# Column means in two float32r passes, and the key-low passes of two heads on separate row halves of TensorE's array

## The chip, the cores and the metric

One core of a Trainium2 chip runs the whole kernel. The metric is the device time of one execution in microseconds, taken as the median of several runs. The engines that matter are TensorE (PE in the profile: matmuls and transposes; PEld: its weight loads), VectorE (DVE), ScalarE (ACT) and GpSimd (POOL). They run side by side and wait for one another only at semaphores. TensorE multiplies a stationary operand, loaded into an array of 128 x 128, with a moving operand of up to 512 columns.

## The reference

Two layers of a decoder trunk over 512 tokens of width 1024, all in float32. In each layer a normalized input is projected once, and four branches read the projection: a short convolution, sparse attention (DSA), a chunkwise linear recurrence (HGRN2) and cross-attention to 256 memory tokens. The branches are lifted to the model's width, gated, summed and projected, and a SwiGLU feed-forward part follows. What the change touches is three things.

```python
def rmsnorm(x, g):
    y = xf * lax.rsqrt(jnp.mean(xf * xf, axis=-1, keepdims=True) + EPS)
    ...
# index scores of the sparse attention, 8 heads of 64, one common key ik:
rel = jax.nn.relu(jnp.einsum('bthd,bsd->bths', iqb, ik) * idx_scale)
score = jnp.einsum('bths,bth->bts', rel, iwb)
...                                   # the 128 best keys of each token
# attention over them, 8 heads of 64, one common key k:
logits = jnp.einsum('bthd,btkd->bthk', qb, k_sel) * att_scale
p = jax.nn.softmax(logits, axis=-1)
...
# HGRN2 output, 4 heads of 128:
o_c = rmsnorm(o_c, hgrn_out_norm) * jax.nn.silu(g_g)
```

## The kernel before

**Float32 by float32r.** TensorE takes operands in float32 or in float32r (a rounded float32). The kernel splits most operands in two float32r parts, `hi` (a ScalarE copy, L97 in the profile, since the helper `A` records every ScalarE instruction) and `lo` (VectorE's difference of the value and `hi`). A product is then the three passes `hi*hi`, `hi*lo`, `lo*hi` (`mm3`, L270 to L272). Weight chunks are split in this way too (L225). These projections are by far the most of the work: 512 columns of activations a pass in `features`, or 256 columns of weights a pass in `tokens`.

**Column means.** Norms over features that lie on the partitions need a mean down the columns of a 128x512 tile. The kernel takes it by a matmul with a constant matrix, `ones_d` (1/1024) or `ones_h` (1/128), in plain float32: `norm_feature` (L301, three times: ahead of each feed-forward part, and between the layers) and the end of each HGRN2 `head` (L972, four heads in two layers). `norm_token` (L309) takes means of the same sums of squares in another form and isn't touched.

**Scores.** `dots` makes the scores of one head for one block of 128 tokens against `n` keys, where `n` is 128 times the block's number (128 to 512). The query tile of a head (`qS` for attention, `iqS` for the index) has `hi` in partitions 0 to 63 and `lo` in 64 to 127, written by `heads_T`. The key's `hi` (`kS[0]`, `ikS[0]`) stands in both halves, written by `twin`; the key's `lo` stands in the lower half only, with zeros in the other, which GpSimd sets. So the first pass (L685) gives `q_hi*k_hi + q_lo*k_hi`, and the second (L686) `q_hi*k_lo`, both over all 128 rows of the array and into one PSUM tile "at". There are two "at" banks. In `select` (blocks 1 to 3) ScalarE reads an index score with Relu, and VectorE adds it up; `attend` (blocks 0 to 3) has VectorE add the mask and take the maximum, and ScalarE the exponential. Then the probabilities are transposed (L709) and multiplied with the values (L715): this product writes two heads' results to the two column halves of the array, 64 columns each.

**Order.** The kernel's generators are woven together by hand (`script`, `weave`): the steps of `select` and `attend` stand between steps of `lift` and of the branches' projections, so that TensorE has matmuls to do while other engines work on a head. The final order on each engine is made at build time by a scheduler that simulates the engines; TensorE then runs its instructions in that order. Other small matmuls in the text below: L937 to L965 (HGRN2 products, of which L939 uses 64 columns) and L331, a transpose of a tile with only four rows (the positions).

Of the kernel before, what the change touches and what calls it, by code (L numbers as in the profile page):

```python
# [13 lines left out]
F32R = mybir.dt.float32r  # L14
I32 = mybir.dt.int32
U8 = mybir.dt.uint8
AF = mybir.ActivationFunctionType
# [4 lines left out]
P = 128  # L22
S = 512
# [5 lines left out]
HD = 64  # L29
# [40 lines left out]
def hybrid_trunk(ctx: ExitStack, tc: tile.TileContext, x, mem, positions, norm_mix, w_in, conv_w,  # L70
# [3 lines left out]
    act, dve, pe, pool = nc.scalar, nc.vector, nc.tensor, nc.gpsimd  # L74

    consts = ctx.enter_context(tc.tile_pool(name="consts", bufs=1))
    start = ctx.enter_context(ExitStack())
# [7 lines left out]
    order = mybir.DependencyInfo(mybir.DependencyClass.NoSync, mybir.DependencyReason.DATA)  # L85
# [4 lines left out]
    def A(dst, src, func, **kw):  # L90
        name = tables.get(func)
        if name is not None and name != table["set"]:
            load = act.preload_act_table_set(name)
            for u in table["users"]:
                tc.add_manual_dep(load.ins, u.name, order, reason="table set")
            table.update(set=name, load=load.ins, users=[])
        i = act.activation(dst, src, func, **kw)  # L97
        if name is not None:
            tc.add_manual_dep(i.ins, table["load"].name, order, reason="table set")
            table["users"].append(i.ins)  # L100
        return i
# [4 lines left out]
    def at_ps():  # L106
        return pat.tile([P, 512], F32, name="at", bufs=AT_BUFS)
# [4 lines left out]
    def f(ap):  # L112
        return ap.bitcast(F32)
# [3 lines left out]
    ones_d = consts.tile([P, P], F32, name="ones_d")  # L117
    dve.memset(ones_d, 1.0 / D)
    ones_h = consts.tile([P, P], F32, name="ones_h")
    dve.memset(ones_h, 1.0 / P)  # L120
    eps = consts.tile([P, 1], F32, name="eps")
    dve.memset(eps, EPS)
    half = consts.tile([P, 1], F32, name="half")
# [18 lines left out]
    ps = tr_ps()  # L142
# [16 lines left out]
    ps = tr_ps()  # L159
# [136 lines left out]
    def scratch512(n):  # L296
        return state.tile([P, S], F32, name="sq", bufs=2)[:, :n]

    def norm_feature(ssq):
        ps = tr_ps()  # L300
        pe.matmul(ps, ones_d, ssq, start=True, stop=True)  # L301
        r = state.tile([P, S], F32, name="rstd", bufs=1)
        rstd(r, ps, scratch512(S), scratch512(S))
        return r
# [196 lines left out]
    def mixer(l, h, norms, cm, cf):  # L501
# [174 lines left out]
        with pool_("dsa") as dp:  # L676
            qS = dp.tile([P, 8, S], F32R, name="qS")
            kS = (dp.tile([P, S], F32R, name="k_hi"), dp.tile([P, S], F32R, name="k_lo"))
            pool.memset(f(kS[1][HD:P, :]), 0.0)
            vt = dp.tile([P, NT, HD], F32, name="vt")  # L680
            biases = [causal_bias] + [dp.tile([P, (t + 1) * P], F32, name=f"bias{t}") for t in range(1, NT)]

            def dots(ps, q, k, hh, t, n):
                s = slice(t * P, (t + 1) * P)
                pe.matmul(ps, q[:, hh, s], k[0][:, :n], start=True, stop=False)  # L685
                pe.matmul(ps, q[:, hh, s], k[1][:, :n], start=False, stop=True)  # L686

            def attend(t, dp2, y_b):
                n = (t + 1) * P
                s = slice(t * P, (t + 1) * P)  # L690
                for q in range(2):
                    probs = []
                    for i in range(4):
                        ps = at_ps()[:, :n]
                        dots(ps, qS, kS, 4 * q + i, t, n)
                        p = dp2.tile([P, S], F32, name="prob", bufs=PR_BUFS)[:, :n]
                        mx, sm = small(1), small(1)
                        dve.tensor_tensor_reduce(out=p, in0=ps, in1=biases[t], scale=-1.0, scalar=-OFF * 4,  # L698
                                                 op0=OP.add, op1=OP.min, accum_out=mx)
                        A(p, p, AF.Exp, bias=mx, scale=-1.0, accum_out=sm)  # L700
                        dve.reciprocal(sm, sm)
                        A(p, p, AF.Copy, scale=sm)
                        probs.append(p)
                    pt = dp2.tile([P, NT, S], F32, name="pt", bufs=PT_BUFS)
                    for b in range(t + 1):
                        pp = tr_ps()
                        for e in range(2):
                            for i in range(2):
                                pe.transpose(pp[:, (2 * e + i) * P:(2 * e + i + 1) * P],  # L709
                                             probs[2 * i + e][:, b * P:(b + 1) * P], ident)  # L710
                        A(pt[:, b, :], pp, AF.Copy)
                    pv = tr_ps()[:, :2 * P]
                    for b in range(t + 1):
                        for e in range(2):
                            pe.matmul(pv[e * HD:(e + 1) * HD, :], vt[:, b, :], pt[:, b, e * 2 * P:(e + 1) * 2 * P],  # L715
                                      start=b == 0, stop=b == t)
                    pv = pv.rearrange("p (a b) -> p a b", b=P)
                    hi, lo = (y_b[x][:, 2 * q:2 * q + 2, s] for x in range(2))
                    A(hi, pv, AF.Copy)
                    dve.tensor_sub(lo, pv, f(hi))  # L720
                    yield

            with pool_("idx") as ip:
                iqS = ip.tile([P, 8, S], F32R, name="iqS")
                ikS = (ip.tile([P, S], F32R, name="ik_hi"), ip.tile([P, S], F32R, name="ik_lo"))
                pool.memset(f(ikS[1][HD:P, :]), 0.0)
                iw = ip.tile([P, NT, 8], F32, name="iw")

                def rope(u, heads, t):
# [21 lines left out]
                def heads_T(dst, h0, u, heads, t):  # L751
                    ps = tr_ps()[:, :heads * HD]
                    for i in range(heads // 2):
                        pe.transpose(ps[:, i * P:(i + 1) * P], u[:, i * P:(i + 1) * P], ident)  # L754
                    ps = ps.rearrange("p (a b) -> p a b", b=P)
                    s = slice(t * P, (t + 1) * P)
                    for e in range(2):
                        d = dst[:, h0 + e:h0 + heads:2, s]
                        src = ps[e * HD:(e + 1) * HD]
                        A(d[0:HD], src, AF.Copy)  # L760
                        dve.tensor_sub(d[HD:P], src, f(d[0:HD]))

                def unit(ps, t, c0, heads):
                    u = ip.tile([P, 4, HD], F32, name="unit", bufs=3)[:, :heads]
# [3 lines left out]
                def twin(ps, t, c0, norm, dst):  # L768
                    u = ip.tile([P, 2, HD], F32, name="twin", bufs=2)
                    A(u[:, 0, :], ps[:, c0:c0 + HD], AF.Copy, scale=r_t[:, t:t + 1])  # L770
                    if norm:
                        headnorm(u[:, 0:1], 1, gk_b[l])
                    rope(u[:, 0:1], 1, t)
                    dve.tensor_copy(u[:, 1, :], u[:, 0, :])
                    ps = tr_ps()[:, :P]
                    pe.transpose(ps, u.rearrange("p a b -> p (a b)"), ident)
                    s = slice(t * P, (t + 1) * P)
                    A(dst[0][:, s], ps, AF.Copy)
                    dve.tensor_sub(dst[1][0:HD, s], ps[0:HD], f(dst[0][0:HD, s]))

                def iq_part(ps, t, c0, heads, h0):
                    u = unit(ps, t, c0, heads)
# [24 lines left out]
                def select(t):  # L807
                    n = (t + 1) * P
                    score = ip.tile([P, S], F32, name="score", bufs=1)[:, :n]
                    for hh in range(8):  # L810
                        ps = at_ps()[:, :n]
                        dots(ps, iqS, ikS, hh, t, n)
                        rel = ip.tile([P, S], F32, name="rel", bufs=2)[:, :n]
                        A(rel, ps, AF.Relu, scale=HD ** -0.5)
                        if hh == 0:
                            dve.tensor_scalar(score, rel, iw[:, t, 0:1], 0.0, op0=OP.mult, op1=OP.add)
                        else:
                            dve.scalar_tensor_tensor(score, rel, iw[:, t, hh:hh + 1], score, op0=OP.mult,
                                                     op1=OP.add)
                    dve.copy_predicated(score[:, t * P:], future, neg)  # L820
                    yield
                    for i in range(TOPK // 8):
                        m8 = ip.tile([P, 8], F32, name="m8", bufs=2)
                        dve.max(m8, score)
                        dve.match_replace(score, m8, score, REPL)
                        if i % 4 == 3:
                            yield
                    dve.tensor_scalar(biases[t], score, REPL, OFF, op0=OP.not_equal, op1=OP.mult)
# [24 lines left out]
        with pool_("hgrn") as hp:  # L853
# [29 lines left out]
            def head(hh):  # L883
# [85 lines left out]
                osq = tmp("e")  # L969
                A(osq, po, AF.Square)  # L970
                pm = tr_ps()
                pe.matmul(pm, ones_h, osq, start=True, stop=True)  # L972
                y, a = tmp("ls"), tmp("ks")
                dve.tensor_mul(zg, zg, po)
                rstd(y, pm, y, a)
# [140 lines left out]
```

## Time and profile before

| | us |
|---|---|
| median of 3 runs | 2047.55 (2047.5 to 2048.2) |
| the profiled execution, its own time | 2047.48 |
| its span, first to last instruction | 2045.4 |
| TensorE busy | 2034.5 |
| TensorE's weight loads busy | 1715.8 |
| VectorE busy | 1269.3 |
| ScalarE busy | 1017.5 |

The profile comes from one execution. "Busy" is the time in which an engine had an instruction in flight; on TensorE matmuls overlap in the pipeline, so a busy TensorE isn't one at its peak. In the timeline each row has the start and the length in us, the engine, the line, the operation, the tiles (output<-inputs), the array's rows*columns for TensorE, the shape, and the count where several alike were merged. In the answers for one line three durations stand for the shortest, the median and the longest, in ns. The page's groups end with "busy, mean ns of one | idle time of the engine just before them, and what ended it".

### The profile page before, as it was taken

The page shows a single profiled execution, that of the slowest core. Times are in us where ns is not written, and L with a number is a line of the kernel's source. Part 1 is how long each engine was busy: PE and PEld are TensorE (multiplying, and loading weights), DVE is VectorE, ACT ScalarE, POOL GpSimd, SP SyncE. Part 2 cuts the span into 40 slices and gives each one's busy share as a digit, 9 for nine tenths or more (in the row PEclk, how much of TensorE's full clock was granted, in tenths as well). Part 3 has the DMA queues.
Part 4 walks back from the last instruction along what each step waited for, and adds up shares of the span by engine and source line. Part 5 has one row for each costly group of instructions (what it writes and reads, how often), then busy time and mean ns, then how long its engine had stood idle before and what let it go on. Part 6 is the DMA issues. An engine that isn't in the chain of part 4 may idle for free.

```text
span 2045.4 us, 26581 instructions
## 1 busy us (share of the span) xinstructions
PE 2034.5 (99%) x10348; PEld 1715.8 (84%) x10348; DVE 1269.3 (62%) x2507; ACT 1017.5 (50%) x1834; POOL 9.8 (0%) x33
## 2 busy tenths in 40 slices
PE   8999999999999999999999999999999999999999
PEld 8998988888888888888889898888888888888887
DVE  6779998547676544334457889963777754533442
ACT  7653655766665423223355456576767633322331
POOL 0000000000000000000000000000000000000000
PEclk9999999999999999999999999999999999999999
DMA  7632232223233232233243213322223322323322
GB/s 253 220 89 94 68 93 93 64 71 93 78 118 113 83 103 93 93 105 102 87 155 94 88 58 107 97 76 63 83 83 101 126 90 96 103 75 111 97 79 93
DMA packets 187709, 203.79 MB, mean 100 GB/s; under 512 B 4270, under 2 KB 176384, under 8 KB 187456
## 3 DMA queue, kind: packets, MB, share of 16 engines
q1 hardware_dynamic: 183872, 193.56, 29.8%
q10 hardware_dynamic: 3552, 8.41, 1.1%
q8 instruction: 81, 1.33, 0.3%
q14 instruction: 44, 0.36, 0.1%
q0 software_dynamic: 160, 0.13, 0.0%
HBM read 191.60 MB, written 10.49 MB: 99 GB/s over the span
## 4 chain that ended last, share of the span: by engine, by line
PE 99%; DMA 1%; DVE 0%; ACT 0%; SPq 0%; issue 0%; DVEq 0%
PE mm L270 30%; PE mm L272 30%; PE mm L271 30%; PE tr L715 1%; PE tr L709 1%; PE at L686 1%; PE at L685 1%; PE at L272 1%; PE at L270 1%; PE at L271 1%; DMA w_raw<-in_mem_w_kv_dram 1%; PE at L963 0%; PE at L937 0%; PE tr L653 0%; PE tr L754 0%; PE tr L972 0%
## 5 line engine op out<-in xcount | busy, mean ns | idle before, releaser
L270 PE MATMUL mm<-h_hi,w_hi 128*128 128x512 f32 x1664 | 653.0, 393 | 0.0
L271 PE MATMUL mm<-h_lo,w_hi 128*128 128x512 f32 x1664 | 652.1, 392 | 0.0
L272 PE MATMUL mm<-h_hi,w_lo 128*128 128x512 f32 x1664 | 650.1, 392 | 0.0
L225 DVE TENSOR_TENSOR w_lo<-w_raw,w_hi 128x1024 fp32r<-128x1024 f32 (+1 forms) x346 | 419.5, 1213 | 364.5 <-ACT w_hi L97 361.3
L97 ACT ACTIVATE w_hi<-w_raw 128x1024 fp32r<-128x1024 f32 (+1 forms) x346 | 363.4, 1051 | 460.8 <-PE mm L271 414.5
L272 PEld LDWEIGHTS mm<-h_hi,w_lo 128*128 128x128 f32 x1664 | 312.8, 188 | 64.8 <-issue 1.2
L270 PEld LDWEIGHTS mm<-h_hi,w_hi 128*128 128x128 f32 x1664 | 312.8, 188 | 64.5 <-issue 2.2
L271 PEld LDWEIGHTS mm<-h_lo,w_hi 128*128 128x128 f32 x1664 | 312.9, 188 | 63.8 <-issue 2.0
L272 PE MATMUL mm<-w_hi,h_lo 128*128 128x256 f32 (+1 forms) x448 | 128.2, 286 | 0.0
L271 PE MATMUL mm<-w_lo,h_hi 128*128 128x256 f32 (+1 forms) x448 | 127.0, 285 | 0.0
L270 PE MATMUL mm<-w_hi,h_hi 128*128 128x256 f32 (+1 forms) x448 | 127.0, 285 | 0.0
L271 PE MATMUL mm<-a_lo,w_hi 128*128 128x512 f32 x272 | 106.3, 391 | 0.0
L270 PE MATMUL mm<-a_hi,w_hi 128*128 128x512 f32 x272 | 106.0, 390 | 0.0
L272 PE MATMUL mm<-a_hi,w_lo 128*128 128x512 f32 x272 | 105.8, 391 | 0.0
L270 PE MATMUL mm<-y_hi,w_hi 128*128 128x512 f32 x256 | 101.4, 397 | 0.0
L272 PE MATMUL mm<-y_hi,w_lo 128*128 128x512 f32 x256 | 100.6, 393 | 0.0
L271 PE MATMUL mm<-y_lo,w_hi 128*128 128x512 f32 x256 | 100.3, 392 | 0.0
L272 PEld LDWEIGHTS mm<-w_hi,h_lo 128*128 128x128 f32 x448 | 85.8, 191 | 1.4 <-issue 0.8
L270 PEld LDWEIGHTS mm<-w_hi,h_hi 128*128 128x128 f32 x448 | 85.3, 191 | 1.2 <-issue 0.8
L271 PEld LDWEIGHTS mm<-w_lo,h_hi 128*128 128x128 f32 x448 | 85.6, 191 | 0.6
L97 ACT ACTIVATE a_hi<-fg 128x512 fp32r<-128x512 f32 x44 | 27.8, 633 | 109.4 <-DVE fg L1065 109.4
L97 ACT ACTIVATE prob<-prob,small 128x128 f32<-128x128 f32 (+3 forms) x128 | 69.2, 554 | 15.2 <-DVE small L698 14.6
(358 smaller groups left out, 2946.9 us busy)
## 6 DMA issues: line engine op xcount, KB each, us to landing
w_raw<-in_w_in_dram SPq DMA_DIRECT2D x72, 1024.0 KB, 5.3
w_raw<-in_ffn_w_up_dram SPq DMA_DIRECT2D x44, 1024.0 KB, 5.1
w_raw<-in_w_lift_dram SPq DMA_DIRECT2D x32, 512.0 KB, 3.5
w_raw<-in_ffn_w_down_dram SPq DMA_DIRECT2D x16, 1024.0 KB, 5.5
w_raw<-in_mem_w_kv_dram SPq DMA_DIRECT2D x8, 1024.0 KB, 5.4
w_raw<-in_w_out_dram SPq DMA_DIRECT2D x8, 1024.0 KB, 5.2
w_raw<-in_ffn_w_down_dram SPq DMA_DIRECT2D x10, 512.0 KB, 3.4
kv<-kv ACTq DMA_DIRECT2D x8, 512.0 KB, 3.2
```

The costliest lines, as they stand in the source:

```text
L97: i = act.activation(dst, src, func, **kw)
L225: dve.tensor_sub(lo, raw[:, k:e], f(hi))
L270: pe.matmul(ps, ah, bh, start=first, stop=False)
L271: pe.matmul(ps, ah, bl, start=False, stop=False)
L272: pe.matmul(ps, al, bh, start=False, stop=last)
L685: pe.matmul(ps, q[:, hh, s], k[0][:, :n], start=True, stop=False)
L686: pe.matmul(ps, q[:, hh, s], k[1][:, :n], start=False, stop=True)
L709: pe.transpose(pp[:, (2 * e + i) * P:(2 * e + i + 1) * P], probs[2 * i + e][:, b * P:(b + 1) * P], ident)
L715: pe.matmul(pv[e * HD:(e + 1) * HD, :], vt[:, b, :], pt[:, b, e * 2 * P:(e + 1) * 2 * P], start=b == 0, stop=b == t)
```

## The change

The column means are split like other operands: `hi` and `lo` of the squares, and two float32r passes with constants that are exact in that form (`column_means`). The matmuls L301 and L972 become two passes each, with one ScalarE copy and one VectorE subtraction ahead of them.

`dots` now makes two heads at once. The first pass of each stays as it was. The second one uses only 64 rows: for the even head of the pair the rows 0 to 63, for the odd head the rows 64 to 127. For that the odd head's query has its `hi` in the upper partitions (64 to 127) and its `lo` in the others, and the key's `lo` now stands in both halves. The two 64-row passes are ordered behind both whole passes. Both "at" banks are taken by one pair. The GpSimd memsets go.

```diff
+    ones_dr = consts.tile([P, P], F32R, name="ones_dr")
+    dve.tensor_copy(ones_dr, ones_d)
+    ones_hr = consts.tile([P, P], F32R, name="ones_hr")
+    dve.tensor_copy(ones_hr, ones_h)
...
+    def column_means(ps, ones, sq, hi, lo):
+        A(hi, sq, AF.Copy)
+        dve.tensor_sub(lo, sq, f(hi))
+        pe.matmul(ps, ones, hi, start=True, stop=False)
+        pe.matmul(ps, ones, lo, start=False, stop=True)
...
     def norm_feature(ssq):
         ps = tr_ps()
-        pe.matmul(ps, ones_d, ssq, start=True, stop=True)
+        column_means(ps, ones_dr, ssq, *(scratch512(S).bitcast(F32R) for _ in range(2)))
...
-            pool.memset(f(kS[1][HD:P, :]), 0.0)
...
-            def dots(ps, q, k, hh, t, n):
+            def dots(q, k, hh, t, n):
                 s = slice(t * P, (t + 1) * P)
-                pe.matmul(ps, q[:, hh, s], k[0][:, :n], start=True, stop=False)
-                pe.matmul(ps, q[:, hh, s], k[1][:, :n], start=False, stop=True)
+                pss = [at_ps()[:, :n] for _ in range(2)]
+                for e in range(2):
+                    whole = pe.matmul(pss[e], q[:, hh + e, s], k[0][:, :n], start=True, stop=False)
+                for e in range(2):
+                    r = slice(e * HD, (e + 1) * HD)
+                    part = pe.matmul(pss[e], q[r, hh + e, s], k[1][r, :n], start=False, stop=True)
+                    tc.add_manual_dep(part.ins, whole.ins.name, order, reason="side by side")
+                return pss
...                                    # in attend, and alike in select
-                        ps = at_ps()[:, :n]
-                        dots(ps, qS, kS, 4 * q + i, t, n)
+                        if i % 2 == 0:
+                            pss = dots(qS, kS, 4 * q + i, t, n)
+                        ps = pss[i % 2]
...                                    # in heads_T
-                        A(d[0:HD], src, AF.Copy)
-                        dve.tensor_sub(d[HD:P], src, f(d[0:HD]))
+                        hi, lo = d[e * HD:(e + 1) * HD], d[(1 - e) * HD:(2 - e) * HD]
+                        A(hi, src, AF.Copy)
+                        dve.tensor_sub(lo, src, f(hi))
...                                    # in twin
-                    dve.tensor_sub(dst[1][0:HD, s], ps[0:HD], f(dst[0][0:HD, s]))
+                    dve.tensor_sub(dst[1][:, s], ps, f(dst[0][:, s]))
...                                    # at the end of an HGRN2 head
-                pe.matmul(pm, ones_h, osq, start=True, stop=True)
+                column_means(pm, ones_hr, osq, *(hp.tile([P, S], F32R, name=nm) for nm in ("osq_hi", "osq_lo")))
```

More of the change, by code (lines that the diff above doesn't have):

```diff
@@ L725, in mixer @@
                 ikS = (ip.tile([P, S], F32R, name="ik_hi"), ip.tile([P, S], F32R, name="ik_lo"))
-                pool.memset(f(ikS[1][HD:P, :]), 0.0)
                 iw = ip.tile([P, NT, 8], F32, name="iw")
@@ L810, in select @@
                     for hh in range(8):
-                        ps = at_ps()[:, :n]
-                        dots(ps, iqS, ikS, hh, t, n)
+                        if hh % 2 == 0:
+                            pss = dots(iqS, ikS, hh, t, n)
+                        ps = pss[hh % 2]
                         rel = ip.tile([P, S], F32, name="rel", bufs=2)[:, :n]
```

## Prediction

> **What bounds the kernel.** I read the page first: busy times, then the chain that ended last.
>
> ```profile
> span 2045.4 us, 26581 instructions
> PE 2034.5 (99%) x10348; PEld 1715.8 (84%) x10348; DVE 1269.3 (62%) x2507; ACT 1017.5 (50%) x1834; POOL 9.8 (0%) x33
> PEclk9999999999999999999999999999999999999999
> PE 99%; DMA 1%; DVE 0%; ACT 0%; SPq 0%; issue 0%; DVEq 0%
> ```
>
> TensorE (PE) is on 99% of the chain; VectorE (DVE) and ScalarE (ACT) are half idle, and the granted clock is flat. Next, the list of who waited for whom, for TensorE alone. These five are the whole list:
>
> ```profile
> PE tr L160 <- DMA rows<-in_mem_k_norm_dram: 1.9, 1, 1.9
> PE mm L271 <- DVE w_lo L225: 1.3, 2, 0.8
> PE tr L144 <- DVE ones_d L118: 1.1, 1, 1.1
> PE mm L270 <- ACT w_hi L97: 1.0, 1, 1.0
> PE tr L386 <- DVE mt_lo L388: 0.8, 2, 0.6
> ```
>
> Together 6.1 us, and their lines are those of the start (constants, memory tokens, first weights). After that TensorE never waits, so a change is worth what it does to TensorE's own sequence, microsecond for microsecond. "Busy" can't price that: a matmul's record includes time in the pipeline, which its successor overlaps. I therefore price an instruction as the step from the end of its predecessor to its own end (start plus duration in the timeline).
>
> **What the column means save.** TensorE's timeline around one mean in the HGRN2 part:
>
> ```profile
> 483.24 0.39 PE L270 MATMUL mm<-y_hi,w_hi 128*128 128x512 f32 x1
> 483.46 0.39 PE L271 MATMUL mm<-y_lo,w_hi 128*128 128x512 f32 x1
> 483.69 0.40 PE L272 MATMUL mm<-y_hi,w_lo 128*128 128x512 f32 x1
> 483.93 1.02 PE L972 MATMUL tr<-e,ones_h 128*128 128x512 f32 x2
> ```
>
> The float32r passes step by 0.225 us. The float32 mean is two records: it ends at 484.95, 0.86 after 484.09, so 0.43 a record. How many there are, from the answers for the two lines:
>
> ```profile
> L972 PE MATMUL tr<-e,ones_h x16: 589/593/596, 483.9 to 1583.4; 128*128 128x512 f32 x16
> L301 PE MATMUL tr<-ssq,ones_d x6: 590/594/676, 700.3 to 1685.4; 128*128 128x512 f32 x6
> ```
>
> 22 records are 11 means. Each becomes two passes of 0.225: 0.86 - 0.45 = 0.41 saved, **4.5 us** in all. What each adds elsewhere is one ScalarE copy and one VectorE subtraction of 128x512, ahead of the second pass. The nearest rows of these shapes, and the last sum ahead of a mean beside the matmul that reads it:
>
> ```profile
> L97 ACT ACTIVATE a_hi<-fg 128x512 fp32r<-128x512 f32 x44 | 27.8, 633 | 109.4 <-DVE fg L1065 109.4
> L1067 DVE TENSOR_TENSOR a_lo<-fg,a_hi 128x512 fp32r<-128x512 f32 x44 | 30.4, 692 | 29.3 <-ACT a_hi L97 29.3
> 1055.50 0.68 DVE L291 TENSOR_TENSOR ssq<-ssq,sq 128x512 f32<-128x512 f32 x1
> 1060.64 0.94 PE L309 MATMUL tr<-ones_d,ssq 128*128 128x1 f32 x8
> ```
>
> That is 0.63 + 0.69 = 1.3 us more per chain. Between layers the sum is ready at 1056.18 and read at 1060.64, so 4.5 us of projections cover it; elsewhere the changed program's instruction order puts 3 to 9 other matmuls between the two passes, except between layers, where they touch. I price it at zero. Without cover it would be 11 x 1.3 = 14 us. The two copies of constants at the start and the two GpSimd memsets that go are a few short instructions on engines that don't bind: zero.
>
> **What the dots save.** The low pass (L686), by size:
>
> ```profile
> L686 PE MATMUL at<-k_lo,qS x64: 220/310/502, 327.1 to 1411.0; 128*128 128x128 f32 x16, 128*128 128x256 f32 x16, 128*128 128x384 f32 x16, 128*128 128x512 f32 x16
> L686 PE MATMUL at<-ik_lo,iqS x48: 278/337/398, 154.6 to 1281.0; 128*128 128x256 f32 x16, 128*128 128x384 f32 x16, 128*128 128x512 f32 x16
> ```
>
> 512 columns step by 0.225, 256 by 0.12 (rows below); for 384 I take 0.17 between them, for 128 something from 0.06 (half of 256) to 0.12, say 0.10. So 32 x (0.225 + 0.17 + 0.12) + 16 x 0.10 = 18.1 us of low passes now.
>
> In the changed program's order the 112 low passes stand as 54 pairs directly behind one another and 4 single ones (two 512-key pairs have an L715 product between their halves). If a pair runs in the time of one pass, what is left is 18 x 0.225 + 16 x 0.17 + 16 x 0.12 + 8 x 0.06 = 9.2 us, and 0.01 for each second half, 0.5. Saved: 18.1 - 9.7 = **8.4 us**. The high passes stay, whole.
>
> **What the dots add: changes of the array's shape.** No 64-row pass is in the trace. The nearest is L715, two 64-column halves side by side:
>
> ```profile
> 399.26 0.28 PE L270 MATMUL mm<-w_hi,h_hi 128*128 128x256 f32 x1
> 399.38 0.28 PE L271 MATMUL mm<-w_lo,h_hi 128*128 128x256 f32 x1
> 399.59 0.65 PE L715 MATMUL tr<-pt,vt 128*64 128x256 f32 x4
> 400.17 0.38 PE L272 MATMUL mm<-w_hi,h_lo 128*128 128x256 f32 x1
> 400.39 0.28 PE L270 MATMUL mm<-w_hi,h_hi 128*128 128x256 f32 x1
> ```
>
> The four records take 399.66 to 400.24, 0.58 us. A float32 record of 256 columns is half of 0.43, so one by one they would take 0.86: halves do overlap, two steps of 0.215. But 0.58 - 0.43 leaves **0.15 us** for going in. Coming back, L272 ends 0.31 after the last of them where the next full pass takes 0.12 (400.55 to 400.67): **0.19 us** for coming out. Does a matmul on fewer rows pay this too? One does exist, four rows high:
>
> ```profile
> 52.28 0.36 PE L271 MATMUL mm<-w_lo,mt_hi 128*128 128x256 f32 x1
> 52.58 0.13 PEld L331 LDWEIGHTS tr<-ident,pos_f 4*128 4x128 f32 x1
> 52.58 0.22 PE L331 MATMUL tr<-ident,pos_f 4*128 4x4 f32 x1
> 52.73 0.19 PEld L272 LDWEIGHTS mm<-w_hi,mt_lo 128*128 128x128 f32 x1
> 52.73 0.38 PE L272 MATMUL mm<-w_hi,mt_lo 128*128 128x256 f32 x1
> 52.84 0.19 PEld L270 LDWEIGHTS mm<-w_hi,mt_hi 128*128 128x128 f32 x1
> 52.95 0.28 PE L270 MATMUL mm<-w_hi,mt_hi 128*128 128x256 f32 x1
> ```
>
> It ends 0.16 after the full pass before it, with next to nothing to stream, and the pass behind it ends 0.31 later, the one after that 0.12: the same two prices. The weight loads show what the price holds: L270's load starts at 52.84, 0.27 before the pass ahead of it ends; L331's and L272's start only 0.06 and 0.07 before that and stand exposed. The Trainium skill ("TensorEngine Tiling (Array Packing)", Tiling Modes) states that changing the tiling mode drains TensorE, while changing the tile does not; it gives no price, and this trace's 0.15 and 0.19 bear it out.
>
> Going into row halves has two ends: 0.15 as in both rows, or 0.20, since the float32r weights of a full load take 0.19 (L272's load) and the loads in those rows 0.13, 0.05 less:
>
> ```profile
> L715 PEld LDWEIGHTS tr<-pt,vt x160: 132/136/138, 358.5 to 1430.3; 128*64 128x64 f32 x160
> ```
>
> I take 0.20, since the new halves are float32r loads of 128 columns like those of 0.19. By the lower end the total below would be 58 x 0.05 = 2.9 us less. The Trainium skill ("TensorE: Matmul & The Clock Gate", LDWEIGHTS) says that a load's time goes by columns and not by rows, which would give the upper end, +8.0 us below.
>
> The count, from the changed program's order: 58 entries into row halves (52 from the full array, 6 from column halves) and 58 exits (52 to full float32r passes, 2 to transposes, 4 to column halves). Column halves are entered 4 times less from the full array, and left towards it 6 times less. Entries 58 x 0.20 = 11.6; exits 52 x 0.19 + 6 x 0.15 = 10.8; the column changes that fall away, 10 x 0.15, -1.5. Sum **+20.9 us**. All of it lies on TensorE's sequence, with nothing to hide behind.
>
> The pair also adds a wait: both "at" banks must be free before its second whole pass, and every projection queued on TensorE stands behind that. Its readers take 0.6 us a bank on ScalarE:
>
> ```profile
> L97 ACT ACTIVATE rel<-at 128x512 f32<-128x512 f32 x16 | 9.5, 595 | 4.5 <-PE at L686 4.4
> ```
>
> Successive pairs stand more than 20 matmuls apart in nearly all places, over 2.4 us at 0.12 each, against 1.2 us for two reads: zero.
>
> **Sum.** 20.9 - 8.4 - 4.5 = +8.0 us; with entries at 0.15, +5.1. The profiled execution took 2047.48 us around its span of 2045.4, and the median of the runs is 2047.55, so one sum serves for both: **2055.5 us**.
>
> **Rivals.**
> *A: the change of shape is free for row halves.* If the loads of row halves slip in under the full pass, the 20.9 us vanish: 2047.5 - 8.4 - 4.5 = 2034.6. It decides below 12.9 / 106 = 0.12 us for each of the 106 added changes (182 against 76). For it: float32r never ran on part of the rows here. Against it: the four-row instruction paid both ways. The Trainium skill ("TensorE: Matmul & The Clock Gate", Part 3) has loads overlap when the row group differs and prices a second tile at about 4 ns, with no term for the way in or out; the rows above contradict the latter. Chance 0.12.
> *B: row halves are not side by side.* If the second half streams after the first, or its load waits for the first one's, 54 pairs lose 14 x 0.225 + 16 x 0.17 + 16 x 0.12 + 8 x 0.06 = 8.3 us less the 0.5: 2063.3; with the loads alone in a row (0.11 each, twice the 0.05 by which a full load exceeds half of one) 2061.4. For it: no row shows two row halves. Against it: column halves overlap. Chance 0.17.
> *C: the price is about half,* 0.10 us a change: 10.6 - 12.9 = -2.3, 2045.2; at 0.14, 2049.4. Chance 0.09, mostly no measurable change.
> The forecast keeps 0.62.
>
> **Numbers.** What can be told from no change here is about 0.2%, 4.1 us. Forecast and B are slower by more than that, but for the forecast's thin lower edge: slower 0.78. A and the lower part of C are faster: 0.14; the rest of C and that edge, 0.08 same. The range takes in the forecast with both entry prices, some luck in the order, and B: 2050 to 2064; A and most of C stay outside.
>
> **What would show it.** In the new trace: the first of each low pair ends about 0.20 us later than its stream explains, its partner 0.01 behind it, and the next full pass steps 0.41 instead of 0.225 (0.31 instead of 0.12 at 256 columns). Each mean should step 0.45, and TensorE should have no new waits behind the start. I am wrong if the low halves' weight loads start while the whole pass before them still streams (A), if partners end a full stream apart (B), or if TensorE waits on a score bank or on a mean's low part.

## Result and profile after

The changed kernel takes 2064.92 us (median of 4 runs, 2064.23 to 2065.45), the kernel before 2047.53 us beside it: 1.0084 times as long (95% interval 1.0072 to 1.0096), 17.4 us slower. The forecast was 2055.5 us, with a range up to 2064. The direction held, the forecast of 8.0 us was less than half of what came, and the range ended 0.9 us short of it.

The page of the changed kernel, against the same lines of before:

```profile
span 2062.9 us, 26610 instructions
PE 2046.4 (99%) x10348; PEld 1709.6 (83%) x10348; DVE 1278.3 (62%) x2520; ACT 1026.4 (50%) x1845; POOL 7.7 (0%) x29
PE 95%; DVE 3%; DMA 1%; ACT 1%; issue 0%; SPq 0%; DVEq 0%; ACTq 0%
```

TensorE is still busy for 99%, but its busy time grew by 11.9 us and the span by 17.5. The chain that ended last now runs for 3% over VectorE and 1% over ScalarE, which showed 0% before: TensorE has begun to wait. How long and for whom is in the list of its waits (total us, times, longest), 11.8 us in all where it was 6.1:

```profile
PE mm L274 <- ACT y_hi L97: 3.3, 3, 2.8
PE tr L164 <- DMA rows<-in_mem_k_norm_dram: 1.8, 1, 1.8
PE mm L275 <- DVE w_lo L229: 1.3, 2, 0.8
PE tr L148 <- DVE ones_d L118: 1.1, 1, 1.1
PE mm L274 <- ACT w_hi L97: 1.0, 1, 1.0
PE tr L727 <- ACT pt L97: 0.9, 2, 0.5
PE tr L396 <- DVE mt_lo L398: 0.8, 2, 0.6
PE at L275 <- DVE mpt_lo L667: 0.7, 2, 0.3
PE mm L275 <- DVE y_lo L674: 0.5, 2, 0.3
PE mm L274 <- DVE fg L1079: 0.4, 2, 0.2
```

The five of the start are the old ones. New are `y_hi` and `y_lo` (a branch's output, read by its lift), `pt` (attention), `mpt_lo` (cross-attention) and `fg` (feed-forward).

The scores themselves behave as forecast. A pair of index scores at 512 keys in TensorE's timeline:

```profile
268.25 0.39 PE L698 MATMUL at<-ik_hi,iqS 128*128 128x512 f32 x1
268.57 0.49 PE L701 MATMUL at<-ik_lo,iqS 64*128 64x512 f32 x2
268.99 0.50 PE L275 MATMUL mm<-h_lo,w_hi 128*128 128x512 f32 x1
269.33 0.39 PE L276 MATMUL mm<-h_hi,w_lo 128*128 128x512 f32 x1
```

The whole pass ends at 268.64, both halves at 269.06, the next full pass at 269.49, the one behind it at 269.72. So two low passes cost 0.42 us, where a stream of 512 columns is 0.225: they run side by side, with 0.20 us for going in. Coming out costs 0.43 - 0.23 = 0.20. Two passes of 0.225 would have been 0.45; the pair with both changes takes 0.62.

A mean's first pass ends 0.22 us behind its neighbour, as priced (495.16 to 495.38):

```profile
494.76 0.40 PE L275 MATMUL mm<-h_lo,w_hi 128*128 128x512 f32 x1
494.99 0.39 PE L306 MATMUL tr<-osq_hi,ones_hr 128*128 128x512 f32 x1
```

I added up every step of TensorE's sequence (end of one matmul to the end of the next) by kind in both traces. Against before, in us: going into row halves +11.3 (58 times 0.19 to 0.20), coming out of row and column halves +9.9, low streams -9.1, whole score passes -0.2, means -4.5, steps longer than their form's usual step **+10.7** (0.6 before, 11.2 now, behind the first 70 us), the rest -0.6. That is +17.5, the growth of the span. I call the long steps the excess; where a step begins to count as long moves it by some tenths. It holds the waits and the slow passes behind them, and it is the part that the prediction had at zero.

Its largest piece lies at the end of layer 1's HGRN2 part:

```profile
1603.53 0.62 ACT L97 ACTIVATE osq_hi<-e 128x512 fp32r<-128x512 f32 x1
1604.18 0.69 DVE L305 TENSOR_TENSOR osq_lo<-e,osq_hi 128x512 fp32r<-128x512 f32 x1 [0.20 <-ACT osq_hi L97]
1608.60 0.39 PE L306 MATMUL tr<-osq_hi,ones_hr 128*128 128x512 f32 x1
1609.30 0.39 PE L307 MATMUL tr<-osq_lo,ones_hr 128*128 128x512 f32 x1
1609.73 0.69 ACT L97 ACTIVATE ls<-tr,eps 128x512 f32<-128x512 f32 x1 [2.91 <-PE tr L307]
1614.05 0.63 ACT L97 ACTIVATE y_hi<-ls 128x512 fp32r<-128x512 f32 x1 [2.21 <-DVE ls L995]
1614.73 0.73 PE L274 MATMUL mm<-y_hi,w_hi 128*128 128x512 f32 x2 [2.76 <-ACT y_hi L97]
```

The operands are ready at 1604.87, but in TensorE's order the mean stands 3.7 us further back. The first matmul that reads what is made from it (`y_hi`) stands only 10 matmuls behind it, 2.3 us, while the chain from mean to `y_hi` takes 5.0. In the order of the kernel before 52 matmuls stood there, and `y_hi` was done 4.3 us ahead of its first reader (the reads of `y_hi` before 1595.88 are of an earlier head):

```profile
1582.99 1.02 PE L972 MATMUL tr<-e,ones_h 128*128 128x512 f32 x2
1590.93 0.61 ACT L97 ACTIVATE y_hi<-ls 128x512 fp32r<-128x512 f32 x1
1595.88 0.62 PE L270 MATMUL mm<-y_hi,w_hi 128*128 128x512 f32 x2
```

In the changed kernel TensorE waits 2.76 us, and what follows is slow too. The windows table (length, then busy time and instructions by engine, the granted clock, DMA) of the wait and the time behind it:

```profile
1611.90:1614.70 2.80, 0.07 (x1) 0.00 (x0) 2.05 (x3) 0.63 (x1) 0.00 (x0) 1.00 0.00 0
1614.70:1619.50 4.80, 4.77 (x12) 3.06 (x13) 3.86 (x6) 1.69 (x2) 0.00 (x0) 0.65 0.59 174
1620.00:1630.00 10.00, 10.00 (x46) 8.24 (x45) 8.73 (x13) 8.88 (x13) 0.00 (x0) 1.00 0.66 220
```

The granted clock falls to 0.65 on average of 4.8 us, and full passes step 0.43 instead of 0.225.

### The profile page after: what moved, and what is told of

The parts are those of the page before. It is cut to its first block, busy times and chain, and to the rows that moved or that the text cites. A ratio compares the mean times of both kernels' runs of the same rounds, so it can differ in the third digit from the quotient of the medians.

```text
span 2062.9 us, 26610 instructions
## 1 busy us (share of the span) xinstructions
PE 2046.4 (99%) x10348; PEld 1709.6 (83%) x10348; DVE 1278.3 (62%) x2520; ACT 1026.4 (50%) x1845; POOL 7.7 (0%) x29
## 4 chain that ended last, share of the span: by engine, by line
PE 95%; DVE 3%; DMA 1%; ACT 1%; issue 0%; SPq 0%; DVEq 0%; ACTq 0%
PE mm L274 29%; PE mm L275 29%; PE mm L276 29%; PE tr L733 1%; PE at L701 1%; PE tr L727 1%; PE at L698 1%; DMA w_raw<-in_mem_w_kv_dram 1%; PE at L276 1%; PE at L274 1%; PE at L275 1%; DVE w_lo L229 1%; DVE m L843 0%; DVE score L844 0%; PE at L956 0%; PE at L982 0%
```

## Experiments

**1. The means alone.** The scores as before, `column_means` at all eleven places:

```diff
...                                    # column_means and its constants, as in the change
-        pe.matmul(ps, ones_d, ssq, start=True, stop=True)
+        column_means(ps, ones_dr, ssq, *(scratch512(S).bitcast(F32R) for _ in range(2)))
...
-                pe.matmul(pm, ones_h, osq, start=True, stop=True)
+                column_means(pm, ones_hr, osq, *(hp.tile([P, S], F32R, name=nm) for nm in ("osq_hi", "osq_lo")))
```

> The column means alone; the scores stay as before. Theory 1: the means save 11 x 0.41 = 4.5 us on TensorE, but their longer chain makes new waits: about 5 us where the last HGRN2 head of layer 1 is lifted (a wait of 3 us and a low TensorE clock behind it) and 0.46 us behind each of the two feed-forward norms. So 2047.5 - 4.5 + 6 = 2049. Rival: these waits come from the pairs of scores, which shift the order of everything behind them; then the means alone give 2043.

Measured: 2049.83 us against 2047.81, 1.0009 (1.0000 to 1.0019), 2.0 us slower, at the edge of what can be told from no difference. TensorE saves its 4.5 us, and the waits eat more:

```profile
PE mm L274 <- ACT y_hi L97: 2.8, 1, 2.8
PE mm L274 <- DVE fg L1070: 0.4, 2, 0.2
1599.70:1604.50 4.80, 4.46 (x12) 2.98 (x13) 3.93 (x6) 1.70 (x3) 0.00 (x0) 0.69 0.62 169
```

The wait of 2.8 us and the low clock behind it (0.69) are here without any row half. Over all steps the excess is 7.3 us, against 0.6 before. The rival, which gave these waits to the pairs, falls.

**2. The pairs alone.** The changed kernel with the float32 means back:

```diff
-        column_means(ps, ones_dr, ssq, *(scratch512(S).bitcast(F32R) for _ in range(2)))
+        pe.matmul(ps, ones_d, ssq, start=True, stop=True)
...
-                column_means(pm, ones_hr, osq, *(hp.tile([P, S], F32R, name=nm) for nm in ("osq_hi", "osq_lo")))
+                pe.matmul(pm, ones_h, osq, start=True, stop=True)
...                                    # column_means and its constants go
```

> The score pairs on row halves alone; the means stay in float32. Theory 1: changes of shape less the saved streams, 20.9 - 8.4 = 12.5 us, and the new waits of the memory branch and of the attention (3.3 + 1.4 us in the changed kernel), which lacks a score bank while a pair holds both: 2064. Rival: all new waits belong to the pairs, that of the last HGRN2 head too: 2070. Second rival: the shape costs nothing and only waits cost: about 2052.

Measured: 2062.84 us, 1.0075 (1.0060 to 1.0090), 15.0 us slower. The two halves of the change add up: 2.0 + 15.0 = 17.0 of 17.4. Its own waits are those of attention and cross-attention, with no 2.8 us:

```profile
PE tr L717 <- ACT pt L97: 0.9, 2, 0.5
PE at L271 <- DVE mpt_lo L657: 0.7, 2, 0.3
PE mm L271 <- DVE y_lo L664: 0.5, 2, 0.3
PE mm L270 <- ACT y_hi L97: 0.5, 2, 0.3
```

The list counts only time with no matmul in flight; by steps the excess is 5.2 us, 4.6 more than before.

**3. Pairs over all rows.** The changed kernel, its low passes whole:

```diff
-                    part = pe.matmul(pss[e], q[r, hh + e, s], k[1][r, :n], start=False, stop=True)
+                    part = pe.matmul(pss[e], q[:, hh + e, s], k[1][:, :n], start=False, stop=True)
```

> The changed kernel, with the low pass of each head over all 128 rows (its query tile whole against the key's low part, which stands in both halves; this adds the product of the two low parts). Pairs, banks and order rules stay; no change of shape. Theory 1: the low passes cost what they did before, so 2047.5 - 4.5 + 10 us of waits = 2053. If the price of the shape were not the cause, it would stay at 2065 or above, since 8.4 us of streams come back.

Measured: 2053.41 us, 1.0027 (1.0016 to 1.0038). The pairing, the banks and the new waits are still there; only the shape is gone:

```profile
267.13 0.39 PE L698 MATMUL at<-ik_hi,iqS 128*128 128x512 f32 x1
267.35 0.62 PE L701 MATMUL at<-ik_lo,iqS 128*128 128x512 f32 x2
267.81 0.40 PE L275 MATMUL mm<-h_lo,w_hi 128*128 128x512 f32 x1
```

Two whole low passes end 0.45 us behind the pass before them, and the pass behind needs 0.24. So row halves as such cost 2064.92 - 2053.41 = 11.5 us net, or 11.8 with each time taken against the kernel before beside it. The forecast's two terms gave 20.9 - 8.4 = 12.5.

**4. One by one.** The low pass of each head right behind its own whole pass:

```diff
-                for e in range(2):
-                    whole = pe.matmul(pss[e], q[:, hh + e, s], k[0][:, :n], start=True, stop=False)
-                for e in range(2):
-                    r = slice(e * HD, (e + 1) * HD)
-                    part = pe.matmul(pss[e], q[r, hh + e, s], k[1][r, :n], start=False, stop=True)
-                    tc.add_manual_dep(part.ins, whole.ins.name, order, reason="side by side")
+                last = None
+                for e in range(2):
+                    r = slice(e * HD, (e + 1) * HD)
+                    whole = pe.matmul(pss[e], q[:, hh + e, s], k[0][:, :n], start=True, stop=False)
+                    if last is not None:
+                        tc.add_manual_dep(whole.ins, last.ins.name, order, reason="one by one")
+                    last = pe.matmul(pss[e], q[r, hh + e, s], k[1][r, :n], start=False, stop=True)
```

> The changed kernel, with each head's 64-row low pass right behind its own whole pass, so that no two stand side by side. Theory 1: 112 entries and exits at 0.40 us, 45 us, no saved streams, the means and their waits as in the changed kernel: 2047.5 + 45 + 2 = 2094, some us more with the banks' waits. Rival: two halves side by side cost the time, by getting in each other's way, and a single one is free: 2050.

Measured: 2091.01 us (one run), 43.2 us slower than before, 3 less than expected. By steps its 112 entries take 21.8 us, where the changed kernel's 58 take 11.3: the price goes with the number of changes of shape, not with two halves being side by side. The expected waits for the banks did not come: though a pair takes both banks here too, the list has no `pt`, no `mpt_lo` and no `y_lo`, and of `y_hi` only the wait of 2.8 us.

**5. Five of the means.** Two passes in layer 0's heads and between the layers only:

```diff
+                if l:
+                    pe.matmul(pm, ones_h, osq, start=True, stop=True)
+                else:
+                    column_means(pm, ones_hr, osq, ...)
...                                    # and norm_feature between the layers
```

> Two-pass means only in the four HGRN2 heads of layer 0 and in the norm between the layers; the other six stay in float32, the scores stay as before. Theory 1 (the longer chain costs only where its reader stands close behind, in layer 1 and ahead of the feed-forward parts): five means save 2.1 us, less 0.6 us for one short wait in layer 0's HGRN2 part and 0.1 us between the layers, 1.4 us faster than before. Rival: the heads' waits come wherever heads are split; then it is 3 us or more slower than before.

Measured: 2046.33 us against 2047.67, 1.3 us faster; the ratio, 0.9994 (0.9984 to 1.0003), doesn't exclude no difference. It excludes the rival's 3 us.

**6. Layer 1's heads only.** The complement for the heads; both norms stay in float32:

```diff
+                if l:
+                    column_means(pm, ones_hr, osq, ...)
+                else:
+                    pe.matmul(pm, ones_h, osq, start=True, stop=True)
```

> Two-pass means only in the four HGRN2 heads of layer 1; all else as before. Theory 1: 1.6 us saved and the wait of about 5 us with the low clock behind it, so 3.4 us slower than before, and the wait of 2.8 us for y_hi in the list. Rival: that wait comes from the shifts of all means together; then it is 1.6 us faster.

Measured: 2050.86 us, 1.0015 (1.0006 to 1.0024), 3.2 us slower. The same split of four means costs nothing that can be told in layer 0 (run 5) and 3.2 us in layer 1. The loss hangs on the place.

**7 and 8. A third score bank,** with the pairs alone and, as a control, in the kernel before:

```diff
-TR_BUFS = 3
-AT_BUFS = 2
+TR_BUFS = 2
+AT_BUFS = 3
```

> The score pairs on row halves alone, with three score banks and two banks for transposes instead of two and three. Theory 1: the 4.7 us of waits in the memory branch and the attention come from a pair holding both score banks; with a third one they go, and it takes 2058 against 2062.8 with two. Rival: they come from the pair's coarser steps whatever the banks, then it stays at 2062 to 2063, or gets longer for the lack of a transpose bank.

> The kernel before with three score banks and two for transposes, as a control for the run with pairs: within 1 us of the kernel before if a transpose bank less costs nothing, more if it does.

Measured: 2068.48 us with the pairs (1.0101, 1.0087 to 1.0115) and 2057.87 us without (1.0049, 1.0036 to 1.0063). The absolute expectation for run 7 failed: the swap of banks costs 10 us by itself, most of it at one wait near 70 us, which both runs have (6.4 us in run 7, 5.8 in run 8). This row of run 8's list shows it:

```profile
PE mm L270 <- ACT ku L97: 6.6, 2, 5.8
```

Against its control the pairs cost 10.6 us, where they cost 15.0 with two banks, 4.4 less. In run 7's list the cross-attention's waits (`mpt_lo`, `y_hi`, `y_lo`) are gone; of attention's, 0.5 of 0.9 us stay:

```profile
PE tr L717 <- ACT pt L97: 0.5, 2, 0.2
```

That speaks for the banks as the cause of most of the 4.6 us. As the orders differ elsewhere too, it isn't a clean separation; and in run 4 these waits are gone with two banks.

**9 and 10. A shorter way to the mean.** The scores as before. In the heads the high part comes straight from PSUM, at raised priority; run 10 also leaves the two feed-forward norms in float32:

```diff
...                                    # column_means in norm_feature, as in run 1 (run 10: between the layers alone)
-                A(osq, po, AF.Square)
-                pm = tr_ps()
-                pe.matmul(pm, ones_h, osq, start=True, stop=True)
+                oh, ol = (hp.tile([P, S], F32R, name=nm) for nm in ("osq_hi", "osq_lo"))
+                pm = tr_ps()
+                with tc.high_priority(offset=AHEAD):
+                    A(oh, po, AF.Square)
+                    A(osq, po, AF.Square)
+                    dve.tensor_sub(ol, osq, f(oh))
+                    pe.matmul(pm, ones_hr, oh, start=True, stop=False)
+                    pe.matmul(pm, ones_hr, ol, start=False, stop=True)
```

> The column means alone, all eleven in two passes, but in the HGRN2 heads the high part is a second Square straight from PSUM, raised in priority together with the low part and the passes; the program then has 52 instead of 10 matmuls between the last head's mean in layer 1 and its first reader. Theory 1: the wait of 2.8 us and the low clock behind it go, and the means keep their 4.5 us less about 1 us of waits behind the feed-forward norms: 2044.2 against 2047.7. Rival: the last head's chain is too long wherever its mean stands; then about 2049 again.

> As the run before, with the two feed-forward norms left in float32, the norm between the layers in two passes. Theory 1: their two passes save 0.41 us each and cost a wait of 0.46 us each, so no difference: 2044.2, give or take 0.3. Rival: the waits are there without the split as well; then this is 0.8 us slower than the run before.

Measured: 2045.15 us for both, against 2047.70: 0.9988 (0.9979 to 0.9997) and 0.9987 (0.9978 to 0.9996), 2.55 us faster than before. Both beat both kernels. The wait for `y_hi` is gone from their lists; what is left in run 9's, apart from the start, is small:

```profile
PE mm L274 <- DVE fg L1075: 0.4, 2, 0.2
PE mm L274 <- DVE gate L548: 0.3, 1, 0.3
```

By steps run 9 has an excess of 2.2 us and run 10 of 1.3, and the means take 0.8 us more in run 10: splitting the feed-forward norms is neither gain nor loss. The times are 0.95 us above expectation, more than the 0.3 us that run 10 was given; another wait in layer 1's HGRN2 part (`gate`, 0.6 us by its step) is a part of that.

## Why the prediction was right and wrong

**Right: what bounds it, and the pricing by steps.** The change did cost what it does to TensorE's own sequence. Low streams -9.1 us (forecast -8.4), means -4.5 (-4.5), going in +11.3 (+11.6, so the upper price of 0.20 was the right choice), coming out +9.9 (10.8 less 1.5). Their sum with the whole passes is +7.4 us, where the forecast was +8.0. The four-row transpose of the kernel before, one instruction, had given the price of a shape that it otherwise never used. The Trainium skill states that a change of tiling mode drains TensorE ("TensorEngine Tiling (Array Packing)", Tiling Modes). The trace agrees: such a change took about 0.20 us each way.

**Rivals.** A (the shape is free) and C (half price) are refuted by runs 3 and 4. B is refuted in its mechanism, since two halves end together (0.42 us for both); its time of 2063.3 was near the result for another reason. That the range, which was stretched to take in B, ended only 0.9 us short is luck.

**Wrong: the two waits priced at zero.** Both steps looked at whether an input comes in time, and not at who stands behind. The two waits that the prediction named as signs of being wrong, on a score bank and on a mean's low part, are not in the new list; those that came stand further on.

*The means' cover ("I price it at zero").* Shown were the sum between the layers and the distance between a mean's two passes (3 to 9 matmuls by the prediction, 2 to 8 in the trace). That cover held: at the end of layer 1's HGRN2 part the operands were ready 3.7 us ahead of the mean. What counted was the distance from a mean to the first reader of what follows from it. In layer 1 the order of the changed program had shrunk it from 52 matmuls to 10. This was to be read before any run in the same list from which the changes of shape were counted. The waits of all means together measured 6 to 7 us (run 1: 7.3 of excess against 0.6), about 5 of them in this one place, more than the means saved. Runs 1 and 6 show that the split in layer 1's heads makes this wait, and runs 9 and 10 that another way of writing the same split avoids it. The bound that the prediction gave, 14 us if all cover were gone, held, but wasn't carried into the range.

*The banks ("against 1.2 us for two reads: zero").* Only successive pairs of scores were weighed, and there zero held. Cross-attention takes its scores and products through the same two banks, and its output is read at once by the first lift. In its last product of each layer 20 matmuls stand between the last transpose and the first reader of `mpt_lo` in the changed order, where the kernel before has 30; TensorE waits there and at the lift. That and the end of attention came to 4.6 us (run 2), so the pairs bring it about. How they do is shown only in part. With a third bank most of it goes (runs 7 and 8). With two banks it goes too, and the distance is 30 again, where each low pass stands right behind its own whole pass (run 4). So taking two banks at once isn't enough; runs 2 and 3 also set both whole passes ahead of the low ones. That fits a pair that holds both banks for longer, but the runs' orders differ elsewhere too, and no run shows that the banks moved the cross-attention in the order.

With 7.4 of sequence and 10.7 of waits and slow steps, less 0.6 elsewhere, the 17.5 us of span are accounted for.

## What to carry to other kernels

Side-by-side halves pay only if the stream they save is longer than the two changes of shape around them: here 0.40 us against 0.225 at best. By these numbers it takes an estimated two pairs of 512 columns in one stay to break even, which no run tried. Where TensorE never waits, a longer chain on idle engines is free only as far as the first reader of its result stands behind it in the final order: count the matmuls between the two, and do it for every user of a buffer that is now held longer. A wait can cost nearly twice its length where the clock falls behind it: the one of 2.76 us came to nearly 5 us of excess in the changed kernel, and to 3.3 in run 3, where the clock stayed up.

## What the runs showed of the hardware

Behind the wait of 2.76 us the granted clock could fall, but didn't always. In the changed kernel's trace it stayed at 1.00 for 1.4 us and was 0.50 for the next 3.3 us, with full passes of 0.43 us instead of 0.225. In run 3's trace the wait is the same, 2.76 us, and the 4.8 us behind it have a clock of 1.00:

```profile
1616.20:1619.50 3.30, 3.30 (x8) 2.10 (x8) 3.17 (x5) 1.69 (x2) 0.00 (x0) 0.50 0.86 253
1604.63 0.73 PE L274 MATMUL mm<-y_hi,w_hi 128*128 128x512 f32 x2 [2.76 <-ACT y_hi L97]
1604.60:1609.40 4.80, 4.46 (x17) 3.08 (x18) 3.97 (x6) 1.70 (x2) 0.00 (x0) 1.00 0.59 178
```

So the length of the wait alone doesn't decide it; what does isn't shown. The ten executions of run 1 fit this: the four with a mean clock of 0.999 took 2048.55 to 2049.26 us, the six with 0.996 to 0.998 took 2049.81 to 2050.71. The shorter new waits, 0.5 us at most in the changed kernel's list, left no slow passes behind them. The load of a row half took 0.18 us in the changed kernel, the load of all rows for the same pass 0.19 in the kernel before, so half the rows save next to nothing in loading:

```profile
L686 PEld LDWEIGHTS at<-k_lo,qS x64: 187/188/246, 326.9 to 1411.0; 128*128 128x128 f32 x64
L701 PEld LDWEIGHTS at<-k_lo,qS x64: 182/183/183, 331.4 to 1435.6; 64*128 64x128 f32 x64
```
